# The last two output blocks of a decoder trunk, taken by token halves

## The chip, the cores and the metric

One core of a Trainium2 chip. The time is that of the core in device microseconds, from the runs of the kernel; the profile is one further execution of the same program, read by the hardware profiler. A core has a matrix engine (TensorE, PE in the profile, with its weight loads as PEld), VectorE (DVE), ScalarE (ACT), GpSimd (POOL) and SyncE (SP), which here only issues transfers. Matrix products go from on-chip memory (SBUF) into PSUM.

## The reference

A trunk of two layers with a token mixer and a gated ConvFFN each, for 256 tokens of 2048 channels in fp32. The part at the end:

```python
h = rms_norm(x, ffn_norm_g[1]) * (1.0 + scale) + shift
u = causal_depthwise_conv(h @ up_w, dw_w, dw_b)          # 2048 -> 2 * 5632, width 3
gt, val = jnp.split(u, 2, axis=-1)
x = x + gate * ((jax.nn.silu(gt) * val) @ down_w)        # 5632 -> 2048
return rms_norm(x, final_norm_g)                         # over the channels of each token
```

The last norm needs, for each token, the mean of the squares of all 2048 channels. It can't be finished for a token before all 16 channel blocks of the down product are there for that token; tokens are independent of one another.

## The kernel before, in words

Everything is kept transposed: channels on the 128 partitions, the 256 tokens along the free dimension. `x` is 16 tiles of 128x256 side by side in one SBUF tile `xall` (`xs[nb]` is tile nb, line 149). A weight matrix is cut into 128x128 blocks. An output tile of 128 channels by 256 tokens is summed in PSUM over the tiles `kt` of the contraction.

fp32 accuracy is made from fp32r products: each operand is split into a high part, rounded to fp32r, and a low part, the rest. One block costs three matmuls, high x high, high x low and low x high (lines 298, 299, 300 in `gemm`). The stationary operand is the weight block, the moving one the activations, 128x256. Each of the three has a weight load of its own, though the first two use the same block.

Weights come in pieces of 8 blocks (512 KB, `load_next`, line 228), issued by SP into a ring of 6 buffers. `split_next` (line 236) makes the high part on ACT (line 244) and the low part on VectorE (line 248) into a ring of 4 pairs, `w_pool`, up to three pieces ahead of the product. The order of the blocks is a list made by `plan` (line 47). For the last product, `down11`, which is the second half of the contraction (22 of the 44 tiles) of layer 1's down projection, the first four output blocks are interleaved, and then each output block follows with its 22 contraction tiles: blocks 14 and 15 are the last 44 entries of the list, so they lie in the last six pieces, 38 to 43.

When an output block is complete, `down_done` (line 985) runs: VectorE adds it, times the gate, to `xs[nb]` (line 987); `Rms.add` (line 390) squares it on ACT (line 393) and adds the square to a running sum on GpSimd (line 397), except for the last block; ACT scales `xs[nb]` by the norm's weight (line 993). After the last block `Rms.rstd` (line 399) sums over the partitions with two fp32 products of a matrix that holds 1/2048 everywhere: one of the running sum (line 401), one of the last square (line 402), both into one PSUM tile. An fp32 product is two passes of TensorE, an fp32r product one. ACT takes the root (line 410).

Then the end of the kernel (lines 1169 to 1181): for each half of 128 tokens, the reciprocal of the root on VectorE (line 1175), and four times a product of it with four tiles of x, 128x512 (line 1178), each followed by its store of 256 KB from SP (line 1180).

The order on the engines is otherwise the program's with priorities; `in_order` (line 196) ties the instructions of each compute engine, from a given place on, to the order in which they stand in the program. Before, it is called at the end of the convolution stage (line 935) and for the end of the kernel (line 1181).

Of the kernel before, what the change touches and what calls it, by code (L numbers as in the profile page):

```python
# [10 lines left out]
F32 = mybir.dt.float32  # L11
F32R = mybir.dt.float32r
AF = mybir.ActivationFunctionType
ALU = mybir.AluOpType
PSUM = bass.MemoryType.PSUM

P = 128
PB = 8
PW = PB * P
# [4 lines left out]
POOL_TAPS = 11  # L24
LATE_POOL, LATE_PE = 10, 8
PRODUCTS = 11

SKEW = {"z": (1, 1), "g0": (1, 1), "g1": (1, 1), "o": (1, 1)}
HEAD = 16
# [12 lines left out]
QUIET = 6  # L42
# [75 lines left out]
def hybrid_trunk(ctx: ExitStack, tc: tile.TileContext, cfg: Cfg, io: dict):  # L118
    nc = tc.nc
    D, T, H = cfg.D, cfg.T, cfg.H  # L120
    KD, KF, CW, FW = cfg.KD, cfg.KF, cfg.CW, cfg.FW
# [7 lines left out]
    w_pool = ctx.enter_context(tc.tile_pool(name="wsplit", bufs=4))  # L129
    tmp = ctx.enter_context(tc.tile_pool(name="tmp", bufs=2))  # L130
    mpool = ctx.enter_context(tc.tile_pool(name="mpool", bufs=3))
# [16 lines left out]
    xall = xpool.tile([P, KD * T], F32, name="x")  # L148
    xs = [xall[:, k * T:(k + 1) * T] for k in range(KD)]
# [5 lines left out]
    ones_d = const.tile([P, P], F32, name="ones_d")  # L155
# [5 lines left out]
    eps_r = const.tile([P, 1], F32, name="eps_r")  # L161
# [16 lines left out]
    fill = []  # L178
    pace = {"rate": 0.0, "credit": 0.0, "side": 0.0, "steps": 0.0, "heads": 2}

    def advance(gens, k):
        for g in list(gens[:k]):
            if next(g, "end") == "end":
                gens.remove(g)
# [11 lines left out]
    def in_order(n0):  # L196

        last = {}
        for ins in list(nc.cur_bb.bb.instructions)[n0:]:
            if ins.engine in last:  # L200
                tc.add_manual_dep(ins, last[ins.engine].name,
                                  mybir.DependencyInfo(mybir.DependencyClass.NoSync, mybir.DependencyReason.DATA),
                                  reason="in_order")
            if ins.engine in (nc.tensor.engine, nc.vector.engine, nc.scalar.engine, nc.gpsimd.engine):
                last[ins.engine] = ins
# [10 lines left out]
    def drain(gens):  # L216
        while gens:
            advance(gens, 1)
# [3 lines left out]
    raws, parts = [], []  # L222
    look = {"at": 0, "load": 1, "split": 1}

    def load(src, dst):
        tc.keep_in_program_order(nc.sync.dma_start(dst, src))

# [8 lines left out]
    def split_next(later=False):  # L236

        blocks, v, n = raws[len(parts)]
        if stream[len(parts)][0] == "pw1":
            parts.append((blocks, v, None))  # L240
            return
        wh = w_pool.tile([P, PW], F32R, name="wh")
        wl = w_pool.tile([P, PW], F32R, name="wl")
        nc.scalar.copy(wh[:, :n], v[:, :n])  # L244
        parts.append((blocks, wh, wl))

        def low():
            nc.vector.tensor_tensor(wl[:, :n], v[:, :n], wh[:, :n].bitcast(F32), op=ALU.subtract)  # L248

        if later:  # L250
            return low
        low()
# [16 lines left out]
                pace["rate"], pace["credit"] = rate  # L269

    def gemm(name, xh, xl, done, after=None, width=None, halves=0, ready=None, quiet=0,
             banks=()):

        set_rate(name)
        left, ps, paired, banks = {}, {}, [], list(banks)
        todo = -(-len(cfg.plans[name]) // PB)
        for nb, _ in cfg.plans[name]:  # L280
            left[nb] = left.get(nb, 0) + 1
        for blocks, wh, wl in pieces(name):
            for b, (nb, kt) in enumerate(blocks):
                while ready and not ready(kt):
                    advance(side, pace["heads"])
                first = nb not in ps
                if first and len(ps) < halves:
                    first = not paired
                    bank = psum_acc() if first else paired.pop()
                    ps[nb] = bank[:, 0:T] if first else bank[:, T:2 * T]  # L290
                    if first:
                        paired.append(bank)
                elif first:
                    ps[nb] = (banks.pop(0) if banks else psum_acc)()[:, :width or T]
                o = ps[nb]
                left[nb] -= 1
                c = slice(b * P, (b + 1) * P)
                nc.tensor.matmul(o, wh[:, c], xh[kt], start=first, stop=False, skip_group_check=halves > 0)  # L298
                nc.tensor.matmul(o, wh[:, c], xl[kt], start=False, stop=False, skip_group_check=halves > 0)  # L299
                nc.tensor.matmul(o, wl[:, c], xh[kt], start=False, stop=left[nb] == 0, skip_group_check=halves > 0)  # L300
                if left[nb] == 0:
                    with tc.high_priority(offset=PRIORITY):
                        done(nb, ps[nb])
            todo -= 1
            if todo < quiet:
                pace["rate"] = 0.0
            (after or tick)()
# [640 lines left out]
        drain(fill)  # L948


    def ffn(i, entry, out):
        m = f"ffn{i}"
        NG = KF // 2 + 1
        with ExitStack() as fs:
            gpool = fs.enter_context(tc.tile_pool(name=f"g{i}", bufs=1))
            if i == 0:
                more["pool"] = fs.enter_context(tc.tile_pool(name="mods", bufs=MORE_MODS))
            gh, gl = [None] * KF, [None] * KF
            pend = {}

            def conv3(ps, nb):
                y = t256()
                w = lambda k: pc(f"fdw{i}", nb * FW + k, 1)
                nc.scalar.activation(y, ps[:, :T], AF.Identity, bias=pc(f"fdb{i}", nb, 1), scale=w(FW - 1))  # L964
                for k in range(FW - 1):
                    s = FW - 1 - k
                    nc.vector.scalar_tensor_tensor(y[:, s:], ps[:, :T - s], w(k), y[:, s:],  # L967
                                                   op0=ALU.mult, op1=ALU.add)
                return y

            def up_done(nb, ps):
                pend[nb] = conv3(ps, nb)
                j = nb % KF
                if not (j in pend and j + KF in pend):
                    return
                yg, yv = pend.pop(j), pend.pop(j + KF)
                s = t256()
                nc.scalar.activation(s, yg, AF.Silu)
                nc.vector.tensor_tensor(s, s, yv, op=ALU.mult)
                gh[j] = skewed(gpool, f"g{i}", 0, f"gh{j % NG}")  # L980
                gl[j] = skewed(gpool, f"g{i}", 1, f"gl{j % NG}")
                nc.scalar.copy(gh[j], s)
                nc.vector.tensor_tensor(gl[j], s, gh[j].bitcast(F32), op=ALU.subtract)

            def down_done(h):
                def done(nb, ps):
                    nc.vector.scalar_tensor_tensor(xs[nb], ps[:, :T], gate(m, nb), xs[nb],
                                                   op0=ALU.mult, op1=ALU.add)
                    if h == 1 and i == 0:
                        out.add(nb)  # L990
                    elif h == 1:
                        out.add(xs[nb])
                        nc.scalar.activation(xs[nb], xs[nb], AF.Copy, scale=pc("fin_g", nb, 1))
                return done

            hh, hl = entry.product(f"up{i}0a", up_done, "silu_and_others")
            gemm(f"up{i}0b", hh, hl, up_done, banks=[psum_b, psum_a])
            gemm(f"up{i}1a", hh, hl, up_done)
            need(m, 2)
            gemm(f"down{i}0", gh, gl, down_done(0))  # L1000
            gemm(f"up{i}1b", hh, hl, up_done)
            act_tables("sqrt_and_others")
            gemm(f"down{i}1", gh, gl, down_done(1), quiet=QUIET)
            drain(fill)

    def mods1():

# [156 lines left out]
    rms = Rms()  # L1164
# [1 line left out]
    drain(fill)  # L1166


    std = rms.rstd(root=True)
    rs = tmp.tile([P, T], F32, name="rstd", bufs=1)  # L1170
    HT = T // 2
    here = len(nc.cur_bb.bb.instructions)
    for h in range(2):
        t = slice(h * HT, (h + 1) * HT)
        nc.vector.reciprocal(rs[:, t], std[:, t])
        v = mpool.tile([P, D], F32, name="mraw")[:, :KD * HT].rearrange("p (k t) -> p k t", k=KD)
        for k in range(0, KD, 4):
            nc.vector.tensor_tensor(v[:, k:k + 4], xall.rearrange("p (k t) -> p k t", k=KD)[:, k:k + 4, t],
                                    rs[:, t].unsqueeze(1).to_broadcast([P, 4, HT]), op=ALU.mult)
            nc.sync.dma_start(io["out"][h * KD // 4 + k // 4].rearrange("p (k t) -> p k t", k=4), v[:, k:k + 4])  # L1180
    in_order(here)

def _cols(v):
    return np.ascontiguousarray(np.asarray(v).reshape(-1, P).T)

# [118 lines left out]
```

## Time and profile before

| | us |
|---|---|
| median of 3 runs | 2307.34 (2305.59 to 2307.86) |
| span of the profiled execution, first to last instruction | 2304.7 |
| PE busy / PEld busy in it | 2270.8 / 2168.1 |
| DVE / ACT / POOL busy | 1736.7 / 1164.4 / 334.6 |
| mean granted TensorE clock | 0.997 |
| bytes read from HBM | 598.58 MB |

The profiled execution has no time of its own beside its span; the runs' median lies 2.6 us above that. In the page's rows, "L298 PE MATMUL ps<-gh,wh 128*128 128x256 x1408" is line, engine, operation, output and inputs, weight size, moving or output size, and count; "gh" and "gl" are the high and low parts of the activations of the down product, "hh" and "hl" those of others, "wh" and "wl" the weights' parts. A row of the timeline begins with start and duration in us; "[1.9 <-ACT t L410]" is idle time of the engine before it and what ended it. The ends of matmuls are modelled, and records of neighbouring matmuls overlap, so that what one costs is read from the distance between starts, not from its duration.

### The profile page before, as it was taken

The numbers are of one execution on the slowest core, as the hardware profiler recorded it, in microseconds if no ns is written. First come the engines' busy times: TensorE is split into PE (matmuls) and PEld (weight loads), VectorE is DVE, ScalarE is ACT, GpSimd is POOL, SyncE is SP. The second block draws the span as 40 slices with busy tenths as digits, with TensorE's granted clock in tenths as the row PEclk, the third lists the DMA queues.
The fourth block names the chain that finished last, engine by engine and source line by source line (L and its number), as shares of the span: only waits on it lengthen the run. The fifth ranks groups of instructions, "written<-read, shape, count | busy, mean of one in ns | idle before, by whom it ended". The sixth has DMA issues, their size and how long they took to land.

```text
span 2304.7 us, 44243 instructions
## 1 busy us (share of the span) xinstructions
PE 2270.8 (99%) x17834; PEld 2168.1 (94%) x17834; DVE 1736.7 (75%) x2386; ACT 1164.4 (51%) x1776; POOL 334.6 (15%) x478
## 2 busy tenths in 40 slices
PE   7999999999999999999999999999999999999997
PEld 5888678999999999999999999999999999999997
DVE  7689968899998899999975555668666545666654
ACT  2056655755543355554465555657555434555443
POOL 4058713200000000002111000121000000000010
PEclk9999999999999999999999999999999999999999
DMA  9988799789999999999854555555555555555553
GB/s 397 417 328 306 272 368 355 272 320 356 358 347 384 363 345 361 355 350 345 304 189 159 165 173 167 172 190 179 190 187 189 187 188 186 190 189 187 190 185 110
DMA packets 139167, 603.56 MB, mean 262 GB/s; under 512 B 15441, under 2 KB 15569, under 8 KB 115153
## 3 DMA queue, kind: packets, MB, share of 16 engines
q1 hardware_dynamic: 120242, 464.42, 56.0%
q0 software_dynamic: 18720, 136.32, 15.8%
q8 instruction: 139, 2.28, 0.4%
q14 instruction: 66, 0.54, 0.1%
HBM read 598.58 MB, written 2.10 MB: 261 GB/s over the span
## 4 chain that ended last, share of the span: by engine, by line
PE 88%; DVE 5%; DMA 4%; ACT 1%; issue 1%; POOL 0%; DVEq 0%; SPq 0%; POOLq 0%; ACTq 0%
PE ps L298 25%; PE ps L299 25%; PE ps L300 25%; PE ps L664 5%; DMA mraw<-in_mt_mix 3%; DVE mraw L331 2%; DVE wl L248 1%; PE ps L1133 1%; PE ps L1131 1%; PE ps L1132 1%; DMA mraw<-in_mt_ffn 1%; PE ps L577 1%; PE auxa L577 1%; DVE hl L382 0%; PE auxb L1132 0%
## 5 line engine op out<-in xcount | busy, mean ns | idle before, releaser
L248 DVE TENSOR_TENSOR wl<-raw,wh 128x1024 fp32r<-128x1024 f32 x688 | 842.9, 1229 | 412.7 <-ACT wh L244 408.0
L244 ACT CAST wh<-raw 128x1024 fp32r<-128x1024 f32 x688 | 719.5, 1048 | 823.9 <-PE ps L299 642.1
L298 PE MATMUL ps<-hh,wh 128*128 128x256 f32 (+1 forms) x3264 | 915.8, 281 | 0.0
L299 PE MATMUL ps<-hl,wh 128*128 128x256 f32 (+1 forms) x3264 | 912.1, 279 | 0.0
L300 PE MATMUL ps<-hh,wl 128*128 128x256 f32 (+1 forms) x3264 | 908.3, 278 | 0.1
L299 PEld LDWEIGHTS ps<-hl,wh 128*128 128x128 f32 x3264 | 617.7, 189 | 0.3
L300 PEld LDWEIGHTS ps<-hh,wl 128*128 128x128 f32 x3264 | 612.8, 188 | 0.7 <-DVE wl L248 0.7
L298 PEld LDWEIGHTS ps<-hh,wh 128*128 128x128 f32 x3264 | 612.7, 188 | 0.3
L299 PE MATMUL ps<-gl,wh 128*128 128x256 f32 x1408 | 396.0, 281 | 0.0
L300 PE MATMUL ps<-gh,wl 128*128 128x256 f32 x1408 | 393.7, 280 | 2.1 <-DVE wl L248 2.1
L298 PE MATMUL ps<-gh,wh 128*128 128x256 f32 x1408 | 394.9, 280 | 0.0
L331 DVE CUSTOM_DVE_ANT_0 mraw<-mraw,csr 128x2048 f32<-128x2048 f32 x152 | 348.2, 2292 | 46.3 <-DMA mraw<-in_mt_mix 30.2
L300 PEld LDWEIGHTS ps<-gh,wl 128*128 128x128 f32 x1408 | 265.5, 189 | 2.3 <-DVE wl L248 2.3
L299 PEld LDWEIGHTS ps<-gl,wh 128*128 128x128 f32 x1408 | 266.5, 189 | 0.0
L298 PEld LDWEIGHTS ps<-gh,wh 128*128 128x128 f32 x1408 | 265.6, 189 | 0.0
L397 POOL TENSOR_TENSOR sumsq<-sumsq,t 128x256 f32<-128x256 f32 x56 | 66.2, 1183 | 879.8 <-ACT t L393 879.5
L664 PE MATMUL ps<-hh,raw 128*128 128x256 f32 x832 | 188.8, 382 | 0.0
L664 PEld LDWEIGHTS ps<-hh,raw 128*128 128x128 f32 x832 | 157.8, 191 | 28.3 <-issue 5.8
L967 DVE SCALAR_TENSOR_TENSOR t<-ps,par,t 128x254 f32<-128x254 f32 x328 | 157.3, 480 | 3.9
L704 DVE SCALAR_TENSOR_TENSOR auxb<-u,cpar,auxb 128x256 f32<-128x256 f32 x297 | 121.6, 483 | 4.5 <-ACT auxb L688 3.7
L839 POOL TENSOR_TENSOR y<-y,hl 128x256 f32<-128x256 f32 x143 | 104.4, 730 | 13.4 <-ACT hl L713 3.3
L964 ACT ACTIVATE t<-ps,par 128x256 f32<-128x256 f32 x164 | 91.9, 560 | 0.0
(247 smaller groups left out, 2270.5 us busy)
## 6 DMA issues: line engine op xcount, KB each, us to landing
raw<-in_w_down SPq DMA_DIRECT2D x176, 512.0 KB, 4.5
mraw<-in_mt_ffn POOLq DMA_DIRECT2D x64, 1024.0 KB, 8.3
raw<-in_w_pw SPq DMA_DIRECT2D x96, 512.0 KB, 8.0
mraw<-in_mt_mix POOLq DMA_DIRECT2D x48, 1024.0 KB, 8.2
raw<-in_w_up01b SPq DMA_DIRECT2D x84, 512.0 KB, 7.0
raw<-in_w_up11b SPq DMA_DIRECT2D x84, 512.0 KB, 3.5
raw<-in_w_up00b SPq DMA_DIRECT2D x80, 512.0 KB, 7.6
raw<-in_w_up10b SPq DMA_DIRECT2D x80, 512.0 KB, 3.5
```

What stands on the lines that cost most here:

```text
L244: nc.scalar.copy(wh[:, :n], v[:, :n])
L248: nc.vector.tensor_tensor(wl[:, :n], v[:, :n], wh[:, :n].bitcast(F32), op=ALU.subtract)
L298: nc.tensor.matmul(o, wh[:, c], xh[kt], start=first, stop=False, skip_group_check=halves > 0)
L299: nc.tensor.matmul(o, wh[:, c], xl[kt], start=False, stop=False, skip_group_check=halves > 0)
L300: nc.tensor.matmul(o, wl[:, c], xh[kt], start=False, stop=left[nb] == 0, skip_group_check=halves > 0)
L331: nc.vector.tensor_tensor_reduce(out=v, in0=v, in1=csr, scale=1.0, scalar=0.0, op0=ALU.mult, op1=ALU.add, accum_out=macc[:, nb:nb + 1])
L397: engine.tensor_tensor(self.sum, self.sum, sq, op=ALU.add)
L664: nc.tensor.matmul(banks[j][:, nb // KD * T:(nb // KD + 1) * T], w[:, b * P:(b + 1) * P], hf[kt], start=first, stop=left[j] == 0, skip_gro ...
L704: nc.vector.scalar_tensor_tensor(conv_ps[j], us[j % UBUFS][:, k:k + T], tap(j, k), conv_ps[j], op0=ALU.mult, op1=ALU.add)
L839: nc.gpsimd.tensor_tensor(ys[c], ys[c], pr, op=ALU.add)
L964: nc.scalar.activation(y, ps[:, :T], AF.Identity, bias=pc(f"fdb{i}", nb, 1), scale=w(FW - 1))
L967: nc.vector.scalar_tensor_tensor(y[:, s:], ps[:, :T - s], w(k), y[:, s:], op0=ALU.mult, op1=ALU.add)
```

## The change

Blocks 14 and 15 of the last product are no longer taken by `gemm`. It hands their weight blocks to a new object, `Last`. The first time through, as the pieces arrive, each block's three matmuls run for tokens 0 to 127 only. The weights of all 44 blocks stay in SBUF: the first two of the six pieces are split into two extra pairs of buffers (pool `late`), the other four stay in the ring, which nothing else needs any more. Then `finish` takes the same blocks for tokens 128 to 255. After half of block 14's contraction it puts in the first half's sum over partitions, root, reciprocal, products and stores. After three quarters of block 15's it starts the second half's sum over partitions. After the last matmul come the second half's residual, square, end of the sum, root, reciprocal, four products and stores. The stores are issued by SP and ACT in turn. All compute instructions from the first block of 14 on are tied to the program's order by `in_order`. The number of columns of each matmul in these two blocks goes from 256 to 128, and the number of matmuls is twice what it was.

```diff
+SPLIT_LAST = 2
...
+    n = -(-KF // 2 * SPLIT_LAST // PB)
+    held = {"at": [("down11", KD * KF // 2 // PB - i) for i in range(n, 4, -1)]}
...
-        wh = w_pool.tile([P, PW], F32R, name="wh")
-        wl = w_pool.tile([P, PW], F32R, name="wl")
+        wh, wl = [(held["pool"] if stream[len(parts)] in held["at"] else w_pool).tile([P, PW], F32R, name=x)
+                  for x in ("wh", "wl")]
...
+                if rest and nb >= KD - SPLIT_LAST:
+                    rest(nb, kt, wh[:, b * P:(b + 1) * P], wl[:, b * P:(b + 1) * P])
+                    continue
...
+    class Last:
...
+        def products(self, h, nb, some, of):
+            t = slice(h * T // 2, (h + 1) * T // 2)
+            for i, (kt, wh, wl) in some:
+                if i == 0:
+                    self.ps = psum_acc()
+                o = self.ps[:, :T // 2]
+                nc.tensor.matmul(o, wh, self.gh[kt][:, t], start=i == 0, stop=False)
+                nc.tensor.matmul(o, wh, self.gl[kt][:, t], start=False, stop=False)
+                nc.tensor.matmul(o, wl, self.gh[kt][:, t], start=False, stop=i == of - 1)
+
+        def block(self, nb, kt, wh, wl):
+            if self.here is None:
+                self.here = len(nc.cur_bb.bb.instructions)
+                self.std = t256()
+                self.rs = tmp.tile([P, T], F32, name="rstd", bufs=1)
+            if not self.blocks or self.blocks[-1][0] != nb:
+                self.blocks.append((nb, []))
+            n, of = len(self.blocks[-1][1]), KF // 2
+            self.blocks[-1][1].append((kt, wh, wl))
+            self.products(0, nb, [(n, (kt, wh, wl))], of)
+            if n == of - 1:
+                self.done(0, nb)
+
+        def done(self, h, nb):
+            t = slice(h * T // 2, (h + 1) * T // 2)
+            nc.vector.scalar_tensor_tensor(xs[nb][:, t], self.ps[:, :T // 2], gate(self.m, nb), xs[nb][:, t],
+                                           op0=ALU.mult, op1=ALU.add)
+            if nb not in self.sq:
+                self.sq[nb] = t256()
+            nc.scalar.activation(self.sq[nb][:, t], xs[nb][:, t], AF.Square)
+            if nb < KD - 1:
+                nc.gpsimd.tensor_tensor(self.rms.sum[:, t], self.rms.sum[:, t], self.sq[nb][:, t], op=ALU.add)
+            nc.scalar.activation(xs[nb][:, t], xs[nb][:, t], AF.Copy, scale=pc("fin_g", nb, 1))
+
+        def sums(self, h, last):
+            t = slice(h * T // 2, (h + 1) * T // 2)
+            if not last:
+                self.ms = psum_b()
+            nc.tensor.matmul(self.ms[:, :T // 2], ones_d, self.sq[KD - 1][:, t] if last else self.rms.sum[:, t],
+                             start=not last, stop=last)
+
+        def scale(self, h):
+            t = slice(h * T // 2, (h + 1) * T // 2)
+            nc.scalar.activation(self.std[:, t], self.ms[:, :T // 2], AF.Sqrt, bias=eps_r)
+            nc.vector.reciprocal(self.rs[:, t], self.std[:, t])
+            v = mpool.tile([P, D], F32, name="mraw")[:, :KD * T // 2].rearrange("p (k t) -> p k t", k=KD)
+            for k in range(0, KD, 4):
+                nc.vector.tensor_tensor(v[:, k:k + 4], self.x[:, k:k + 4, t],
+                                        self.rs[:, t].unsqueeze(1).to_broadcast([P, 4, T // 2]), op=ALU.mult)
+                (nc.scalar if k // 4 % 2 else nc.sync).dma_start(
+                    io["out"][h * KD // 4 + k // 4].rearrange("p (k t) -> p k t", k=4), v[:, k:k + 4])
+
+        def finish(self):
+            for nb, blocks in self.blocks:
+                some, of = list(enumerate(blocks)), len(blocks)
+                first, last = nb == KD - SPLIT_LAST, nb == KD - 1
+                at = of // 2 if first else of * 3 // 4
+                self.products(1, nb, some[:at], of)
+                if first:
+                    self.sums(0, False)
+                    self.sums(0, True)
+                    self.scale(0)
+                if last:
+                    self.sums(1, False)
+                self.products(1, nb, some[at:], of)
+                self.done(1, nb)
+            self.sums(1, True)
+            self.scale(1)
+            in_order(self.here)
...
-            gemm(f"down{i}1", gh, gl, down_done(1), quiet=QUIET)
-            drain(fill)
+            if i == 0:
+                gemm(f"down{i}1", gh, gl, down_done(1), quiet=QUIET)
+                drain(fill)
+            else:
+                held["pool"] = fs.enter_context(tc.tile_pool(name="late", bufs=2))
+                last = Last(m, gh, gl, out)
+                gemm(f"down{i}1", gh, gl, down_done(1), quiet=QUIET, rest=last.block)
+                assert not fill
+                last.finish()
...
-    std = rms.rstd(root=True)
-    rs = tmp.tile([P, T], F32, name="rstd", bufs=1)
-    HT = T // 2
-    here = len(nc.cur_bb.bb.instructions)
-    for h in range(2):
-        t = slice(h * HT, (h + 1) * HT)
-        nc.vector.reciprocal(rs[:, t], std[:, t])
...
-    in_order(here)
```

More of the change, by code (lines that the diff above doesn't have):

```diff
@@ L271, in gemm @@
     def gemm(name, xh, xl, done, after=None, width=None, halves=0, ready=None, quiet=0,
-             banks=()):
+             banks=(), rest=None):
         set_rate(name)
@@ L948, in hybrid_trunk, with __init__ @@
         drain(fill)
+    class Last:
+        def __init__(self, m, gh, gl, rms):
+            self.m, self.gh, self.gl, self.rms = m, gh, gl, rms
+            self.blocks, self.here, self.sq = [], None, {}
+            self.x = xall.rearrange("p (k t) -> p k t", k=KD)
+        def products(self, h, nb, some, of):
[62 more added lines that the diff above has]
+            in_order(self.here)
@@ L1166, in hybrid_trunk @@
     drain(fill)
-    std = rms.rstd(root=True)
-    rs = tmp.tile([P, T], F32, name="rstd", bufs=1)
-    HT = T // 2
-    here = len(nc.cur_bb.bb.instructions)
-    for h in range(2):
-        t = slice(h * HT, (h + 1) * HT)
[L1175 to L1180, printed above, removed]
-    in_order(here)
 def _cols(v):
```

## The prediction

> **What bounds the kernel now.** I read the page first, then the time split into windows around the end, then the chain of waits behind the last matmul, and last the records of TensorE for any matmul of 128 moving columns, because that is the width the change goes to.
>
> ```profile
> span 2304.7 us, 44243 instructions
> PE 2270.8 (99%) x17834; PEld 2168.1 (94%) x17834; DVE 1736.7 (75%) x2386; ACT 1164.4 (51%) x1776; POOL 334.6 (15%) x478
> ...
> PE 88%; DVE 5%; DMA 4%; ACT 1%; issue 1%; POOL 0%; DVEq 0%; SPq 0%; POOLq 0%; ACTq 0%
> ```
>
> TensorE is busy 99% of the span and carries 88% of the chain. But its weight loads (PEld) are busy 94% as well, so a matmul that streams less may not be a shorter matmul.
>
> The three windows are the two blocks before the last two, the last two blocks (the part that the change touches), and everything after the start of the last matmul:
>
> ```profile
> core 0: us, PE busy (x) PEld busy (x) DVE busy (x) ACT busy (x) POOL busy (x), PEclk, DMA share, GB/s
> 2260.48:2275.96 15.48, 15.48 (x134) 15.48 (x133) 7.12 (x8) 7.84 (x10) 2.13 (x2) 1.00 0.31 103
> 2275.96:2291.44 15.48, 15.48 (x134) 15.48 (x133) 4.44 (x5) 3.74 (x6) 1.48 (x2) 1.00 0.00 1
> 2291.44:2304.70 13.26, 1.41 (x7) 0.60 (x5) 7.29 (x11) 1.40 (x3) 0.00 (x0) 0.67 0.43 158
> ```
>
> A block is 22 tiles of the contraction, each three matmuls of 256 columns, so two blocks are 132 matmuls (134 records touch the window, two of them cut by its edges). PE is busy throughout: 15.48 / 132 = 0.1173 us for each matmul, at a granted clock of 1.00. Behind the last matmul lie 13.26 us in which TensorE does almost nothing. The chain of waits runs through these records of VectorE (with the stores' issues on SP), ACT and TensorE:
>
> ```profile
> 2291.76 0.48 DVE L987 SCALAR_TENSOR_TENSOR x<-ps,v_ffn,x 128x256 f32<-128x256 f32 x1 [7.26 <-PE ps L300]
> 2294.11 0.95 DVE L1175 RECIPROCAL rstd<-t 128x128 f32<-128x128 f32 x1 [1.87 <-ACT t L410]
> 2295.09 2.50 DVE L1178 TENSOR_TENSOR mraw<-x,rstd 128x512 f32<-128x512 f32 x4
> 2297.51 0.94 DVE L1175 RECIPROCAL rstd<-t 128x128 f32<-128x128 f32 x1
> 2298.49 2.50 DVE L1178 TENSOR_TENSOR mraw<-x,rstd 128x512 f32<-128x512 f32 x4
> ...
> 2295.81 5.54 SPq L1180 DMA_DIRECT2D out<-mraw  x8
> ```
>
> ```profile
> 2292.33 0.42 ACT L393 ACTIVATE t<-x 128x256 f32<-128x256 f32 x1 [6.78 <-DVE x L987]
> 2292.78 0.51 ACT L993 ACTIVATE x<-x,par 128x256 f32<-128x256 f32 x1
> 2293.60 0.47 ACT L410 ACTIVATE t<-auxb,eps_r 128x256 f32<-128x256 f32 x1 [0.31 <-PE auxb L402]
> ```
>
> ```profile
> 2292.80 0.70 PE L402 MATMUL auxb<-t,ones_d 128*128 128x256 f32 x2 [0.65 <-ACT t L393]
> ```
>
> In order of time: residual, square, sum over partitions, square root; then for each token half a reciprocal and four products. The start of each step is the end of the one before, and the stores run beside the products. The first half's share of this serial end is 2297.51 - 2294.11 = 3.40 us. That is what the change can hide.
>
> **What the change removes from the end.** The first half's reciprocal, four products and stores move beside matmuls: 3.40 us gone from the tail, nearly exactly, because the second half keeps the same shapes (128x128 and 128x512). The other four steps of the tail shrink from 256 to 128 columns. For ACT the same kind of operation stands in both widths, and for the fp32 sum there is a pair of passes with 128 columns:
>
> ```profile
> L713 ACT ACTIVATE hl<-u,cpar 128x256 f32<-128x256 f32 x175 | 73.4, 495 | 0.0
> ```
>
> ```profile
> L693 ACT ACTIVATE hl<-hl,cpar 128x128 f32<-128x128 f32 x8 | 3.0, 387 | 0.0
> ```
>
> ```profile
> 1227.36 0.39 PE L1096 MATMUL auxb<-e,v 128*128 128x128 f32 x2
> 1227.58 0.39 PE L1097 MATMUL auxb<-e,v 128*128 128x128 f32 x2
> ```
>
> ACT saves 0.11 on the square and 0.11 on the root; the sum saves 0.70 - 0.39 = 0.31; the residual (0.48, no row of half its width) saves between 0 and 0.24, and I take 0.13, close to ACT's share. Together 0.66, bounded by 0 and by half of all four (1.04). The removed tail is 3.40 + 0.66 = 4.06 us (3.40 to 4.44). From the last product to the span's end nothing changes, except that every other store is issued by ACT instead of SP. ACT has no issue in this trace. SP's eight take 5.54 us in all, spread by the products they wait for, so the queue itself is no limit; I count nothing and keep -0.3 to +0.7.
>
> **What it adds on TensorE.** Each of the 132 matmuls becomes two of 128 columns, so 264, and each has its own weight load. If time went by columns, this would be free. The rows that decide it come from the attention, where two fp32r matmuls of 128 columns stand among wide ones; first TensorE, then its loads:
>
> ```profile
> 1468.28 0.22 PE L1085 MATMUL auxb<-mh,ones_r 128*128 128x128 f32 x1
> 1468.34 0.28 PE L1086 MATMUL auxb<-ml,ones_r 128*128 128x128 f32 x1
> 1468.45 0.34 PE L298 MATMUL ps<-oh,wh 128*128 128x256 f32 x1
> 1468.63 0.28 PE L299 MATMUL ps<-ol,wh 128*128 128x256 f32 x1
> ```
>
> ```profile
> 1468.29 0.19 PEld L1086 LDWEIGHTS auxb<-ml,ones_r 128*128 128x128 f32 x1
> 1468.39 0.19 PEld L298 LDWEIGHTS ps<-oh,wh 128*128 128x128 f32 x1
> 1468.50 0.19 PEld L299 LDWEIGHTS ps<-ol,wh 128*128 128x128 f32 x1
> 1468.63 0.19 PEld L300 LDWEIGHTS ps<-oh,wl 128*128 128x128 f32 x1
> ```
>
> The recorded start of L1086 follows L1085 by only 0.06 us, as columns alone would have it. But the loads do not follow: from L1086's on they start 0.10, 0.11 and 0.13 apart, and the matmul that comes next is late by as much (L298 to L299 is 0.18, not 0.1173; L1086's and L298's records are 0.06 longer than their kind). The time that two narrow matmuls seemed to save is given back at once. L1086 also uses the same weights as L1085 and still loads them. A matmul of four columns shows the load alone:
>
> ```profile
> 289.64 1.06 PE L593 MATMUL auxb<-cst,rows 128*128 128x4 f32 x8
> ```
>
> ```profile
> 289.64 0.97 PEld L593 LDWEIGHTS auxb<-cst,rows 128*128 128x128 f32 x8 [0.84 <-issue]
> ```
>
> Eight loads in 0.97, less the last one's own 0.19, are seven steps of 0.111 us, with hardly a column to stream. So 128x128 weights cost about 0.111 us a piece, just under the 0.1173 that 256 columns take: the present matmuls barely cover their load, and narrower ones can't. I take 0.111 (bounds 0.105, between the two shorter steps of the attention, and 0.1173, at which a narrow matmul is as slow as a wide one). 264 x 0.111 = 29.30 us against 15.48: **+13.82 us** (+12.2 to +15.5).
>
> The first half's sum over partitions is two fp32 products, the early part of the second half's sum a third, each two passes: 6 passes x 0.111 (0.22 between L1096 and L1097 for two) = **+0.67** in the stream (0.4 to 0.9). Before, the early part of the sum ran while VectorE took the last residual, so nothing is given back for it.
>
> **What lies beside it.** The held weights cost no copy, since only two of the six pieces get other buffers. In the first-half pass a piece of eight lasts 24 x 0.111 = 2.7 us, as before (24 x 0.1173 = 2.8), and its two splitting steps fit:
>
> ```profile
> 2278.95 1.23 DVE L248 TENSOR_TENSOR wl<-raw,wh 128x1024 fp32r<-128x1024 f32 x1 [1.49 <-ACT wh L244]
> ```
>
> ```profile
> 2280.40 1.05 ACT L244 CAST wh<-raw 128x1024 fp32r<-128x1024 f32 x1 [1.07 <-PE ps L299]
> ```
>
> ```profile
> 2285.15 0.73 POOL L397 TENSOR_TENSOR sumsq<-sumsq,t 128x256 f32<-128x256 f32 x1 [6.29 <-ACT t L393]
> ```
>
> The order on every engine is now fixed from the first of the two blocks on, so a wait stalls what is queued behind it. TensorE's sum of the first half waits for the last square of the first half (residual and square, under 0.48 + 0.42 us) behind 33 matmuls, 3.7 us: covered. Behind it VectorE has root, reciprocal and products, 0.36 + 0.95 + 2.50 = 3.8 us and the waits between them, and the residual of block 14's second half queues after them; that block's matmuls end 33 x 0.111 = 3.7 us after the sum, so it may be half a microsecond late, and its square's addition on POOL (at most 0.73) is wanted only 48 matmuls, 5.3 us, later. ACT's issues wait for VectorE's products and hold up only that same square. If this cover were lost, at most the 3.40 of hidden work would come back.
>
> **The sum.** +13.82 + 0.67 - 4.06 = **+10.4 us**, bounds +7.9 to +13.7. The profiled span becomes 2315.1. The median of the runs is 2307.34, that is 2.6 above the span of the profiled one, and I let that stand: **2317.8 us**, +0.45%. The bounds make 2315.2 to 2321.0 of it; with the runs' own scatter (2305.59 to 2307.86) the forecast's own range is 2314 to 2321.5.
>
> [...]
>
> **The rivals.** *Column time decides (not slower).* In a long stream the loads run ahead and each narrow matmul costs the 0.06 us between the recorded starts of L1085 and L1086: 264 x 0.06 = 15.84, so +0.36 + 0.67 - 4.06 = -3.0, or 2304.3. It decides if a load's step falls below about 0.07 us. For it: that gap. Against: the lateness behind it, and L593's steps. Chance 0.07. [...]
>
> *Half of the loads are covered.* The recorded starts from L1085 to L298 average 0.17 / 2 = 0.085 us; if that went on, 264 take 22.4, and the sum is +7.0 + 0.67 - 4.06 = +3.6, or 2310.9. Against it: L298 starts late in truth, as its longer record says. Chance 0.05. [...]
>
> *The repeated load is dropped* (two of three matmuls share the high weights): 176 loads at 0.111 = 19.5, sum +0.7, 2308.0. Against it, line 299 has a load for each matmul today (below). Chance 0.01.
>
> ```profile
> L299 PEld LDWEIGHTS ps<-gl,wh x1408: 187/188/330, 668.0 to 2291.2; 128*128 128x128 f32 x176
> ```
>
> *The clock drops, since the array now idles half the time.* The granted clock of the idle tail is 0.67; at that clock 29.30 us become 43.7, another +14.4, or 2332. Against it, TensorE's queue has no gap there; the eight matmuls of L593 are too few to show more. Chance 0.03.
>
> **How the numbers follow.** The measurement can tell about 0.2%, 4.6 us, from no change. Forecast 0.83 and clock rival 0.03 are slower: 0.86. The other three lie within 4.6 us: 0.13. Faster by over 4.6 needs the column rival and a tail gain beyond its bound: 0.01. If the forecast holds, its own range misses perhaps one time in ten, which leaves 0.75 inside; so the range reaches down to the second rival: 2310.9 to 2321.5.
>
> **What would show it.** Right: 264 matmuls with 128 columns in the last stretch, their loads 0.105 to 0.117 apart, about 29 us for the two blocks where there were 15.5; the first four products and stores beside them, no stall of TensorE at the sums; about 9.2 us from the last matmul to the end. The number of PE instructions goes from 17834 to 17970. Wrong: starts of narrow matmuls 0.06 to 0.09 apart in a row, or a granted clock below 1.00 in that stretch; a tail still of 12 us or more would mean the overlap failed.

## The result, and the profile after

The changed kernel took 2318.50 us (median of 5 runs, 2317.20 to 2320.42) against 2307.86 before (2305.59 to 2308.87): ratio 1.0048, 95% interval 1.0037 to 1.0058. It is slower, by about 10.6 us. Its page, the span, the engines and the queues:

```profile
span 2318.7 us, 44516 instructions
...
PE 2286.0 (99%) x17970; PEld 2183.2 (94%) x17970; DVE 1736.0 (75%) x2388; ACT 1165.7 (50%) x1781; POOL 332.3 (14%) x479
...
q10 hardware_dynamic: 576, 1.05, 0.1%
```

PE has 136 instructions more (17970 for 17834) and is busy 15.2 us longer; VectorE, ACT and GpSimd do what they did. q10 is the new queue, for the four stores that ACT issues.

The two spans differ by more than the medians do, because they are single executions: 3.4 us of the difference were already there before the two blocks begin. They arose about 354 to 365 us into the span, in the product `pw2` (lines 942 and 943 of the kernel before), which the change doesn't touch. So everything below is measured on the **stretch**, from the start of block 14's first matmul to the end of the span, in one profiled execution of each kernel. Parts of the stretch that a run leaves alone repeat to 0.01 us: the matmuls of the two blocks took 15.37 in another run too, the end 13.28 (both below). Here are its windows, after the change: blocks 14 and 15 in both passes, then what lies behind the start of the last matmul. Columns are as before: busy time of each engine, granted clock, DMA share, GB/s.

```profile
2279.51:2309.50 29.99, 29.99 (x271) 29.99 (x270) 5.77 (x10) 3.43 (x9) 1.64 (x3) 1.00 0.10 36
2309.50:2318.72 9.22, 0.76 (x5) 0.43 (x4) 3.80 (x6) 1.08 (x3) 0.00 (x0) 0.72 0.31 114
```

The same two windows of the kernel before, cut at the starts of the first and the last matmul:

```profile
2276.07:2291.44 15.37, 15.37 (x133) 15.37 (x132) 4.33 (x5) 3.74 (x6) 1.48 (x2) 1.00 0.00 1
2291.44:2304.72 13.28, 1.41 (x7) 0.60 (x5) 7.29 (x11) 1.40 (x3) 0.00 (x0) 0.67 0.43 158
```

So the stretch went from 28.65 to 39.21 us, +10.56: +14.62 in the stream of matmuls and -4.06 behind it. (In the expectations below the stretch before is 28.7, counted from one matmul earlier.) VectorE's timeline over the same time:

```profile
2294.40 0.35 DVE L991 SCALAR_TENSOR_TENSOR x<-ps,v_ffn,x 128x128 f32<-128x128 f32 x1 [7.02 <-PE ps L974]
2299.04 0.95 DVE L1010 RECIPROCAL rstd<-t 128x128 f32<-128x128 f32 x1 [4.29 <-ACT t L1009]
2300.03 2.50 DVE L1013 TENSOR_TENSOR mraw<-x,rstd 128x512 f32<-128x512 f32 x4
2302.45 0.34 DVE L991 SCALAR_TENSOR_TENSOR x<-ps,v_ffn,x 128x128 f32<-128x128 f32 x1
2309.81 0.35 DVE L991 SCALAR_TENSOR_TENSOR x<-ps,v_ffn,x 128x128 f32<-128x128 f32 x1 [7.02 <-PE ps L974]
2311.49 0.95 DVE L1010 RECIPROCAL rstd<-t 128x128 f32<-128x128 f32 x1 [1.32 <-ACT t L1009]
2312.47 2.50 DVE L1013 TENSOR_TENSOR mraw<-x,rstd 128x512 f32<-128x512 f32 x4
```

The first half's reciprocal and products now stand at 2299 to 2302.5, beside matmuls, and only one of each is left behind the last matmul. The square, the sum over partitions and the root of the second half follow the residual there:

```profile
2310.20 0.31 ACT L995 ACTIVATE t<-x 128x128 f32<-128x128 f32 x1 [6.51 <-DVE x L991]
...
2311.08 0.37 ACT L1009 ACTIVATE t<-auxb,eps_r 128x128 f32<-128x128 f32 x1
```

```profile
2310.56 0.49 PE L1004 MATMUL auxb<-t,ones_d 128*128 128x128 f32 x2 [0.79 <-ACT t L995]
```

The change does what it says. What it costs is seen in the weight loads of the same stream:

```profile
2284.87 0.19 PEld L973 LDWEIGHTS ps<-gl,wh 128*128 128x128 f32 x1
2284.98 0.19 PEld L974 LDWEIGHTS ps<-gh,wl 128*128 128x128 f32 x1
2285.09 0.19 PEld L972 LDWEIGHTS ps<-gh,wh 128*128 128x128 f32 x1
2285.21 0.19 PEld L973 LDWEIGHTS ps<-gl,wh 128*128 128x128 f32 x1
2285.32 0.19 PEld L974 LDWEIGHTS ps<-gh,wl 128*128 128x128 f32 x1
2285.43 0.19 PEld L972 LDWEIGHTS ps<-gh,wh 128*128 128x128 f32 x1
```

Five steps in 0.56 us, 0.112 each, where a matmul of twice the columns took 0.1173. TensorE is busy for all of the 29.99 us, at the sums too.

### The profile page after: what moved, and what is told of

The parts are those of the page before. It is cut to its first block, busy times and chain, and to the rows that moved or that the text cites. A ratio compares the mean times of both kernels' runs of the same rounds, so it can differ in the third digit from the quotient of the medians.

```text
span 2318.7 us, 44516 instructions
## 1 busy us (share of the span) xinstructions
PE 2286.0 (99%) x17970; PEld 2183.2 (94%) x17970; DVE 1736.0 (75%) x2388; ACT 1165.7 (50%) x1781; POOL 332.3 (14%) x479
## 4 chain that ended last, share of the span: by engine, by line
PE 88%; DVE 5%; DMA 4%; ACT 1%; issue 1%; POOL 0%; SPq 0%; DVEq 0%; POOLq 0%; ACTq 0%
PE ps L305 25%; PE ps L306 25%; PE ps L307 25%; PE ps L671 5%; DMA mraw<-in_mt_mix 3%; DVE mraw L338 2%; DVE wl L252 1%; PE ps L1223 1%; PE ps L1224 1%; PE ps L1225 1%; DMA mraw<-in_mt_ffn 1%; PE auxa L584 1%; PE ps L584 1%; PE ps L973 0%; PE ps L974 0%
## 5 line engine op out<-in xcount | busy, mean ns | idle before, releaser
L306 PE MATMUL ps<-gl,wh 128*128 128x256 f32 x1364 | 383.7, 281 | 0.0
L307 PE MATMUL ps<-gh,wl 128*128 128x256 f32 x1364 | 381.5, 280 | 2.0 <-DVE wl L252 2.0
L305 PE MATMUL ps<-gh,wh 128*128 128x256 f32 x1364 | 382.6, 281 | 0.0
L307 PEld LDWEIGHTS ps<-gh,wl 128*128 128x128 f32 x1364 | 257.2, 189 | 2.4 <-DVE wl L252 2.4
L306 PEld LDWEIGHTS ps<-gl,wh 128*128 128x128 f32 x1364 | 258.2, 189 | 0.0
L305 PEld LDWEIGHTS ps<-gh,wh 128*128 128x128 f32 x1364 | 257.4, 189 | 0.0
```

## The experiments

The theory: a narrow matmul costs its weight load, 0.111 us, so that twice the matmuls cost nearly twice the time, and the shorter end gives back 4.06 of it. Rivals: the loss comes from the fixed order, the sums in the stream or the second pass; or narrow fp32r matmuls stream more slowly.

**The narrow matmuls alone.** In the kernel before, line 298 to 300 run once for each half in these two blocks; nothing else changes.

```diff
+                narrow = name == "down11" and nb >= KD - 2
+                for t in ((slice(0, T // 2), slice(T // 2, T)) if narrow else (slice(0, width or T),)):
...
+                    nc.tensor.matmul(o[:, t], wh[:, c], xh[kt][:, t], ...)
```

> The kernel before, with one part of the change alone: each matmul of blocks 14 and 15 becomes two of 128 columns, one half right behind the other, same residual, norm and end as before. Stretch from the first matmul of block 14 to the end of the span. Theory, weight loads: 264 x 0.111 = 29.3 and the old tail of 13.26, so 42.6 (+13.8 over before). Rival, it isn't the width but the fixed order and the sums in the stream that cost: 28.7, as before.

Its two windows:

```profile
2275.43:2304.75 29.32, 29.32 (x266) 29.32 (x264) 4.33 (x5) 3.94 (x6) 1.46 (x2) 1.00 0.01 1
2304.75:2318.03 13.28, 1.46 (x7) 0.65 (x6) 7.29 (x11) 1.40 (x3) 0.00 (x0) 0.70 0.43 158
```

The stretch is 42.60, 13.95 over before, all of it in the stream, with the old end unchanged. So 263 steps of 0.1115 us. The same columns in twice as many matmuls make the loss; order, sums and second pass are not needed for it.

**The overlap alone.** The changed kernel with matmuls of 256 columns in one pass, and the first half's norm put in half a block into block 14. What the last two blocks add to the first half is left out of that norm.

```diff
-            t = slice(h * T // 2, (h + 1) * T // 2)
+            t = slice(0, T)
...
+            if first and n == of // 2:
+                self.sums(0, False)
+                self.sums(0, True)
+                self.scale(0)
```

> The other part alone: matmuls of 256 columns as before, but the first half's norm, products and stores stand in the stream, half a block into block 14, as in the changed kernel they stand half a block into its second pass. For that it leaves out, for the first token half, the last two blocks' contribution (residual, squares, scale by the norm's weight). Stretch from the first matmul of block 14 to the end of the span. Theory: 15.5 of matmuls, 0.7 of sums, 9.2 behind the last matmul, 25.3, so 3.4 under before (28.7). Rival, the end is not shortened, since the stores or VectorE end as late: 28.7.

```profile
2274.94:2291.02 16.08, 16.08 (x140) 16.08 (x138) 5.42 (x8) 3.07 (x6) 1.20 (x2) 1.00 0.18 66
2291.02:2300.29 9.27, 0.76 (x5) 0.36 (x3) 3.80 (x6) 1.08 (x3) 0.00 (x0) 0.79 0.30 113
```

25.35: the stream 0.71 longer for the sums, the end 4.01 shorter. The gain is real, and the two parts add: 13.95 + 0.71 - 4.01 = 10.65, against 10.56 for the whole change.

**One block instead of two.**

```diff
-SPLIT_LAST = 2
+SPLIT_LAST = 1
```

> Only block 15 is taken by halves; block 14 goes through the ordinary path. Stretch from the first matmul of block 14 to the end of the span. Theory, cost per narrow matmul: 66 x 0.1173 = 7.7 for block 14, 132 x 0.111 = 14.7 for block 15, 0.7 for the sums in the stream, 9.2 behind the last matmul: 32.3, which is 3.6 over before (28.7) and 6.9 under the changed kernel (39.2). Rival, the loss is a fixed one of the second pass, the fixed order or the held weights: about 39, no matter how many blocks are split.

```profile
2276.20:2299.19 22.99, 22.99 (x205) 22.99 (x204) 7.73 (x11) 4.83 (x9) 1.47 (x2) 1.00 0.03 10
2299.19:2308.53 9.34, 0.76 (x5) 0.43 (x4) 4.11 (x7) 1.08 (x3) 0.00 (x0) 0.62 0.55 203
```

32.33, as the theory has it: the cost goes with the number of narrow matmuls, and the end is nearly as short. Even one block gains nothing: 3.7 over before. The 0.12 us more in the end are ACT's, whose issue of the first half's last store now reaches past the last matmul and holds up the square behind it, as its timeline shows (in the changed kernel the square starts 0.39 us behind the residual's start, here 0.50):

```profile
2298.42 1.54 ACTq L1015 DMA_DIRECT2D out<-mraw  x2
2300.01 0.31 ACT L995 ACTIVATE t<-x 128x128 f32<-128x128 f32 x1 [3.94 <-DVE x L991]
```

**Fewer loads for the same halves.** High and low activations side by side in one tile, so that the high weights stream 2 x 128 columns after one load.

```diff
+                nc.tensor.matmul(o.rearrange("p (a t) -> p a t", a=2), wh, self.pairs[kt][:, :, t], ...)
+                nc.tensor.matmul(o[:, :T // 2], wl, self.gh[kt][:, t], ...)
```

> The changed kernel with the same halves and the same columns streamed, but one weight load less for each block and half: the high and the low part of the activations lie side by side in one tile, and the high weights stream both halves' 128 columns as one matmul of 256; their two sums stand in separate PSUM columns and are added by a second residual step. 176 loads instead of 264. Stretch from the first matmul of block 14 to the end of the span. Theory, loads set the step: 88 x 0.1173 + 88 x 0.111 = 20.1, sums 0.7, end 9.2 + 0.4 for the second residual: 30.3. Rival, the loss lies in what is done by halves, not in the number of loads: 39, as in the changed kernel.

```profile
2275.46:2296.28 20.82, 20.82 (x183) 20.82 (x182) 6.83 (x13) 3.44 (x9) 1.65 (x3) 1.00 0.14 52
2296.28:2305.83 9.55, 0.71 (x4) 0.37 (x3) 4.15 (x7) 1.08 (x3) 0.00 (x0) 0.63 0.29 110
```

30.37 for 30.3. With the same columns and a third fewer loads the stream is 9.17 us shorter than in the changed kernel (20.82 for 29.99). So what is paid for goes by the number of matmuls with their loads, not by columns. A load and its matmul can't be counted apart here, since each matmul has a load of its own (17970 of both in the changed kernel). That it is the load rests on how long loads of different widths last in the kernel before:

```profile
L577 PEld LDWEIGHTS auxa<-mraw,hot 128*32 128x32 f32 x80 | 2.1, 108 | 2.8 <-issue 1.9
```

A load of 32 columns lasts 108 ns, one of 128 columns 188 to 189 ns (line 298 to 300). An estimate from these rows: 96 columns more take 0.08 us, so all 128 about 0.107, which is nearly the whole step of 0.1115. No run here leaves the load out of a narrow matmul.

**64 columns.** This was to part the load from a slow stream: 0.111 us for 128 columns is near the 0.117 that a stream at half the speed of the 256-column matmuls would need, an estimate from their 0.1173 us each; 64 columns would then take about half of that.

```diff
+                c = T // 2 if i in (0, of - 1) else T // 4
+                o, t = self.ps[:, :c], slice(h * T // 2, h * T // 2 + c)
```

> The changed kernel, but in the two last blocks all matmuls except those of the first and last contraction tile stream 64 columns instead of 128 (half of the tokens' contributions are left out there). Measured is the stretch from the first matmul of block 14 to the end of the span: 39.2 us in the changed kernel, 28.7 before. Theory, the weight load sets the step (0.111 us whatever the columns): the stretch stays at 39.2, within 0.6, and loads remain 0.111 apart. [...]

Three windows of it: the first 5.24 us of the stream, the rest of the stream, the end:

```profile
2277.23:2282.47 5.24, 5.24 (x50) 5.24 (x48) 1.35 (x2) 0.92 (x2) 0.73 (x1) 1.00 0.01 3
2282.47:2329.69 47.22, 47.22 (x224) 47.22 (x223) 4.51 (x8) 2.50 (x7) 0.91 (x2) 0.50 0.06 23
2329.69:2339.36 9.67, 1.21 (x4) 0.72 (x4) 3.80 (x6) 1.08 (x3) 0.00 (x0) 0.50 0.29 108
```

The forecast of the stretch did not hold: 62.13. In the first window the theory is right: from 2277.23 to 2282.47 the loads make 47 steps of 0.1115 us, though all but the first contraction tile's matmuls stream half the columns, so the slow stream is out. But then the granted clock falls from 1.00 to 0.50, and the loads to this:

```profile
2299.71 0.33 PEld L973 LDWEIGHTS ps<-gh,wh 128*128 128x128 f32 x1
2299.93 0.33 PEld L974 LDWEIGHTS ps<-gl,wh 128*128 128x128 f32 x1
2300.14 0.33 PEld L975 LDWEIGHTS ps<-gh,wl 128*128 128x128 f32 x1
```

The window's 223 loads stand 0.212 us apart on the mean (47.22 us), 1.9 times as far: what sets the step slowed with TensorE's granted clock (0.50 for 1.00).

**96 columns.** The same edit with 96 in place of 64, to see how near 128 columns are to that fall.

> As the run with 64 columns, with 96 (a quarter of the tokens' contributions of a half are left out in all but the first and last contraction tile). With 64 columns the granted clock fell to 0.50 about 5 us into the stretch and the loads went from 0.111 to 0.213 us apart; with 128 it stayed at 1.00. [...] Theory A, the clock falls only when the array is idle most of the time, as at 64: loads stay 0.111 apart, stretch 39.2. Theory B, 128 columns are close to the edge: the clock falls here too, loads 0.213 apart, stretch near 62.

```profile
2279.73:2283.19 3.46, 3.46 (x34) 3.46 (x33) 1.35 (x2) 0.93 (x2) 0.73 (x1) 1.00 0.02 5
2283.19:2333.82 50.63, 50.63 (x240) 50.63 (x239) 4.50 (x8) 2.50 (x7) 0.91 (x2) 0.50 0.06 21
```

The clock falls here too, 3.46 us into the stream, and the stretch is 63.75. Theory B: the edge lies between 96 and 128 columns (0.50 at 96, 1.00 throughout at 128). Where between wasn't tried, and 64 and 96 columns ran once each.

**Halves without extra loads.** If loads are what is paid, the halves should be the stationary operand: the activations of 128 tokens are loaded, and the weights of both blocks, 256 columns, stream. That needs the two blocks' weights side by side in the list, and the result turned back.

```diff
+                nc.tensor.matmul(o, self.gh[kt][:, t], wh, start=i == 0, stop=False)
+                nc.tensor.matmul(o, self.gl[kt][:, t], wh, start=False, stop=False)
+                nc.tensor.matmul(o, self.gh[kt][:, t], wl, start=False, stop=i == KF // 2 - 1)
...
+            for b in range(2):
+                nc.tensor.matmul(self.pt[:, b * P:(b + 1) * P], y[b], ident, start=True, stop=True)
```

> The halves without the extra loads: for blocks 14 and 15 the operands change places, so that the activations of 128 tokens are the stationary operand and the weights of both blocks, 256 columns, the moving one; 132 matmuls as before. The result comes out with tokens on the partitions, is copied to SBUF by ACT and VectorE and turned by two fp32 products with an identity, then normed as in the changed kernel. Stretch from the first matmul of block 14 to the end of the span. Theory: 132 x 0.1173 = 15.5; in the stream two turns and four sums, 12 passes x 0.111 = 1.3; the end is 9.2 plus copy 0.3, turns 0.5 and part of a second residual and square 0.4: 10.4. Sum 27.2, 1.5 under before. Rival, copy and turn cost the end more than the first half's norm is worth: 28.7 or more.

```profile
2274.52:2291.26 16.74, 16.74 (x146) 16.74 (x144) 5.71 (x10) 2.71 (x8) 0.74 (x1) 1.00 0.07 26
2291.26:2301.92 10.66, 1.84 (x11) 1.22 (x9) 4.35 (x8) 1.78 (x6) 0.00 (x0) 0.75 0.42 158
```

27.40, that is 1.25 under before: stream +1.37, end -2.62. In its end VectorE's copy of block 15 waited for ACT's copy of block 14 out of the same PSUM tile:

```profile
2291.87 0.29 DVE L991 COPY turn<-ps 128x128 f32<-128x128 f32 x1 [0.78 <-ACT turn L990]
```

One copy by ACT for both was run eleven times:

```diff
-            nc.scalar.copy(y[0], self.ps[:, :P])
-            nc.vector.tensor_copy(y[1], self.ps[:, P:2 * P])
+            nc.scalar.copy(y, self.ps[:, :2 * P])
```

> The swapped kernel, in which VectorE's copy waited for ACT's copy of the same PSUM tile (0.27 + 0.29 us one behind the other): here ACT copies both blocks in one step, 0.37 for 256 columns. Theory: 0.2 us less in the end than the swapped kernel's 27.4, so 27.2 for the stretch, 1.5 under before; the median of the runs 0.0 to 0.2% under before, which the runs' scatter may hide. Rival, the turn of block 14 starts later by as much as block 15's starts earlier: 27.4.

```profile
2274.70:2291.44 16.74, 16.74 (x146) 16.74 (x144) 5.42 (x9) 2.82 (x8) 0.74 (x1) 1.00 0.07 26
2291.44:2302.08 10.64, 1.74 (x11) 1.15 (x9) 4.06 (x7) 1.89 (x6) 0.00 (x0) 0.78 0.42 158
```

27.38: the rival, nothing gained over two copies. The runs gave a median of 2307.12 beside 2307.82 for the kernel before, ratio 0.9999, 95% interval 0.9990 to 1.0008. The stretch is 1.27 us shorter in the trace; in the time of the whole kernel that can't be told from no change.

**GpSimd takes a product of the end.** In the swapped kernel one of the last four products, in the kernel before one of each four:

```diff
+                eng = nc.gpsimd if h and k == 8 else nc.vector
```

> The swapped kernel, and of the last four products one runs on GpSimd beside VectorE's three. A GpSimd product of 128x256 took 0.73 to 1.06 us, so 1.5 to 2.1 for 128x512, beside 1.9 on VectorE: theory 0.4 to 0.6 under the swapped kernel, 26.7. Rival, GpSimd slows VectorE or ends later itself: no better than the swapped kernel.

> The kernel before, with nothing of the change, but in each half one of the four products on GpSimd. Theory: VectorE has two products of 0.61 less in the serial end, 27.6 for the stretch instead of 28.7. Rival, GpSimd ends its last product later than VectorE its three, or slows it: 28.2 or more.

The swapped kernel's VectorE and GpSimd in the end, and VectorE's two groups in the other:

```profile
2297.36 2.96 DVE L1026 TENSOR_TENSOR mraw<-x,rstd 128x512 f32<-128x512 f32 x3
```

```profile
2297.41 1.77 POOL L1026 TENSOR_TENSOR mraw<-x,rstd 128x512 f32<-128x512 f32 x1 [18.44 <-DVE rstd L1022]
```

```profile
2295.78 2.96 DVE L1179 TENSOR_TENSOR mraw<-x,rstd 128x512 f32<-128x512 f32 x3
...
2299.64 2.96 DVE L1179 TENSOR_TENSOR mraw<-x,rstd 128x512 f32<-128x512 f32 x3
```

Both theories failed and the rivals held: three products on VectorE take 2.96 us beside GpSimd, more than the 2.50 of four without it. One of the three takes the whole excess, 1.75 us for 0.68:

```profile
2297.97 1.75 DVE L1026 TENSOR_TENSOR mraw<-x,rstd 128x512 f32<-128x512 f32 x1
```

The stretches were 28.52 and 30.25, in each case longer than without GpSimd (27.40 and 28.65; the kernel before's matmuls of the two blocks took 15.37 again). In the swapped kernel that is 1.12 us: the last store is issued 0.46 later behind the start of the products (3.00 for 2.54), and from it to the end of the span it is 0.66 longer (4.38 for 3.72). ACT's first issue starts 2.39 behind the start of the products (2299.75), where without GpSimd it was 1.33 (2296.99 for 2295.66).

## Why the prediction was right, point by point

- **The cost on TensorE.** Forecast 264 x 0.111 = 29.30 and 0.67 for the sums, 29.97 in all; the stream is 29.99. Against before that is +14.62 for a forecast +14.49; the small rest is the step of 0.1115. The reading that carried it was of a handful of rows: in the attention, where the start of a narrow matmul seems early, the load behind it tells what is paid, and the eight loads of line 593 gave the size. The run with narrow matmuls alone shows that they make up 13.95 of the 14.62 (the sums are the rest), the runs with one block and with fewer loads that it goes by number.
- **The gain behind the last matmul.** Forecast 4.06, measured 13.28 - 9.22 = 4.06. Hidden were 3.40 for the first half's reciprocal and products. The rest, by the distances between starts, is 0.18 for the narrower residual, 0.11 for the square, 0.28 for the sum and 0.10 for the root, where 0.13, 0.11, 0.31 and 0.11 were forecast; that the total agrees to the last digit is luck. The first half's steps were covered as worked out; the second half's residual of block 14 started at 2302.45, right behind the products, and held up nothing.
- **The sum.** Forecast +10.4, the stretch +10.56, the medians +10.64. The forecast time of 2317.8 is the median before plus the sum, since the 2.6 us between span and median are only taken off and put back; the measured median lies 0.7 above it, 0.5 of which is that the median before is now 2307.86, over five runs. The interval of the ratio allows anything from 8.5 to 13.4 us, so that the medians agree this closely is partly luck. The stretch carries the agreement.
- **The rivals.** Column time and half-covered loads are excluded by a mean step of 0.1115 over 263 steps, and the dropped load by the count of 17970 loads for 17970 matmuls.
- **What was misjudged.** The clock rival was given 0.03, with the argument that TensorE's queue has no gap. That argument is wrong: at 64 and 96 columns the records had no gap either (5.24 us busy of 5.24, 3.46 of 3.46), and the granted clock fell to 0.50. The forecast held because at 128 columns it stayed at 1.00, which nothing in the profile of before showed: in this the prediction was lucky.

By these steps the idea could at best have come out about even in this form; this is an estimate, and no run here splits fewer tiles than one block. Splitting one contraction tile of a block costs 6 x 0.112 - 3 x 0.1173 = 0.32 us, and the matmuls of its second half hide at most 3 x 0.112 = 0.34 us of the first half's norm. Cost and cover grow together, however few tiles are split, and the sums in the stream (0.71) cost what the narrower end steps give (0.66).

## What to carry to other kernels

Halving the columns need not shorten a matmul: here one of 128 columns took 0.1115 us and one of 256 columns 0.1173, and the steps of the narrow ones were those of their weight loads. Before halving the moving side, look at how far apart the loads stand where the program already has a narrow matmul, and go by the loads' starts, not the matmuls'. To split work by tokens without more matmuls, let the split side be the stationary operand and keep the streamed side wide; here the result then had to be turned back, and 1.25 us of the stretch were left, too little to see in the time of the kernel. And check what the hidden work is worth against what the cover costs: here an end shorter by 4 us was bought with 14 us of matmuls.

## What the runs showed of the hardware that was not expected

- **The clock fell at 96 and 64 columns though TensorE's records show no gap before it.** With 128 columns for each load the granted clock stayed at 1.00 over the whole stream (29.99 us), with 96 it fell to 0.50 after 3.46 us and with 64 after 5.24 us, and stayed there. The loads then stood 0.212 us apart on the mean in both runs (47.22 us for 223 loads, 50.63 for 239) instead of 0.1115, and the stretch grew from 39.2 to 63.75 and 62.13 us. TensorE's records leave no gap in either run before the fall (5.24 busy of 5.24 us, 3.46 of 3.46), so a stream of matmuls without a gap was not enough to keep the clock. That the streamed columns count is the reading these two runs suggest, not one they prove. The flag `skip_group_check`, which they have and the changed kernel's matmuls lack, is not the cause: the run with narrow matmuls alone has it too and kept 1.00.
- **GpSimd beside VectorE.** A product of 128x512 took 1.77 us on GpSimd, and VectorE's products of the same shape went from 2.50 us for four to 2.96 us for three beside it. One of the three took 1.75 us and the others 0.68 to 0.69, so VectorE seems to have stood still for about 1.07 us, and was not slowed evenly. What held it is not shown.
